# A host layout by channel for the input of a two-layer encoder kernel, with token norms from TensorE sums

## Chip, cores and metric

The kernel runs on one core of a Trainium2 chip. The metric is the device time of one execution in microseconds (us); for the kernel before it is 1353.13 us, the median of 3 runs (1353.13 to 1354.86).

## What is computed

A trunk of two layers on 1040 tokens (16 learned meta tokens ahead of 1024 inputs, the padding in front of them left out by the kernel) of 1024 channels, in float32. The first layer is a gated DeltaNet: a token norm, one projection to queries, keys, values, gate and two small per-head vectors (b and a), a causal convolution of 4 taps per channel, SiLU, and a chunkwise recurrence. The second is a multi-head latent attention. The change concerns the first lines:

```python
def rms_norm(x, g):
    xf = x.astype(jnp.float32)
    y = xf * lax.rsqrt(jnp.mean(xf * xf, -1, keepdims=True) + EPS)
    return (y * g.astype(jnp.float32)).astype(x.dtype)

def deltanet_layer(x, valid, g_norm, w_in, conv_w, a_log, dt_bias, o_gain, w_out):
    ...
    h = jnp.where(valid[None, :, None], rms_norm(x, g_norm), 0)
    z = h @ w_in
    qkv = jax.nn.silu(causal_dwconv(z[..., :2 * DN_KW + DN_VW], conv_w))
    gate = z[..., 2 * DN_KW + DN_VW:2 * DN_KW + 2 * DN_VW]
    b_raw = z[..., 2 * DN_KW + 2 * DN_VW:2 * DN_KW + 2 * DN_VW + DN_HEADS].astype(jnp.float32)
    a_raw = z[..., 2 * DN_KW + 2 * DN_VW + DN_HEADS:].astype(jnp.float32)
    ...
```

## The kernel before

The normalised input is held by channel: `hT_hi` and `hT_lo` hold, for each of 8 channel tiles of 128 (`kt`), all 1040 tokens. Each number is split into a high part that TensorE takes in its rounded float32 type and a low remainder; a product of two split operands is three TensorE products (`mm3`, lines 91 to 93). The tokens go in three chunks, `TOKC`, of 272, 384 and 384.

*The input stage (lines 215 to 259).* Ten small loads on SP's queue bring x for the first tiles and the norm gains and convolution taps; a TensorE transpose turns these parameters into columns (`pcol`, line 237). For each of 9 token tiles (16 tokens, then 8 of 128) ScalarE squares and sums (`xs`, line 250, through `act`, line 82), a short Newton step on VectorE and ScalarE gives the inverse root (`rsqrt`, lines 173 to 178), and Pool scales the rows (line 252). Then, for each chunk and channel tile, TensorE transposes (line 258), ScalarE writes the high part (line 110) and VectorE the low part (line 111), both with the gain.

*The a/b projection and the gates (lines 261 to 337).* 48 products (lines 274, 275) on all chunks, then a short row of steps on VectorE and ScalarE, and the decay sums on TensorE (lines 325 to 328).

*The projection columns.* `load_w` (line 197) loads a column of 128 outputs in two halves into `raw` (two buffers); Pool writes its high part `whi` (line 98) and VectorE its low part `wlo` (line 99), two buffers each. `conv_acts` multiplies one column with the three chunks (24 x 3 products), ScalarE copies to `z` (line 370, two buffers), Pool and VectorE convolve (lines 372, 375), ScalarE applies SiLU. The order of the columns is keys of heads 0 and 1, values 0 and 1 (one buffer for their result), queries 0 and 1, and so on by pairs of heads. Between them stands the key preparation of a pair (lines 385 to 465, with products of keys with keys at line 440 and masks from Pool at line 429), and the inverse of small blocks on VectorE (line 519 on).

*What sets the order.* A scheduler orders each engine's instructions when the kernel is built, by the program's order and by what it expects to be ready; on the chip each engine takes its instructions in that order. SP's queue issues all loads and stores in its own order, and a load whose buffer is not free holds those behind it. ScalarE has two tables in use, one for Ln and Exp and one for SiLU; `act` orders the steps so that a table is changed only where the program's order changes it: no SiLU of the keys before the gates' last Exp, and no Ln or Exp of the key preparation before the keys' last SiLU.

Of the kernel before, what the change touches and what calls it, by code (L numbers as in the profile page):

```python
# [23 lines left out]
P = 128  # L24
D = 1024
# [14 lines left out]
PART = count()  # L40
TOKC = [(0, 272), (272, 656), (656, 1040)]
# [75 lines left out]
def body(ctx: ExitStack, tc: tile.TileContext, I, out):  # L117
# [37 lines left out]
    off = {}  # L155
    pcol = ctile("pcol", [P, P])

    def col(key, k=0):
        c = off[key] + k
        return pcol[:, c:c + 1]  # L160
# [21 lines left out]
    with ExitStack() as la:  # L182
# [12 lines left out]
        w_in = I["a_w_in"][0].rearrange("(kt p) c -> p kt c", p=P)  # L195

        def load_w(c0):
# [16 lines left out]

        with ExitStack() as l0:
            xp = l0.enter_context(tpool(name="x0", bufs=2))

            def load_x(t):
                a, b = tok(t)
                xt = xp.tile([P, D], F32, tag="xt", name=nm("xt"), bufs=3)  # L220
                SY.dma_start(xt[:b - a], I["meta_tokens"] if t < 0 else I["x"][0, t * P:(t + 1) * P, :])
                return xt

            xts = {t: load_x(t) for t in (-1, 0, 1)}
            n = 0
            prow = xp.tile([P, P], F32, tag="prow", name="prow", bufs=1)
            for key, src, k in (("a", I["a_norm"][0], 8), ("kv", I["kv_norm"], 8), ("b", I["b_norm"][0], 8),
                                ("og", I["a_o_gain"][0], 1), ("gl", I["kv_latent_norm"], 2),
                                ("gq", I["b_q_latent_norm"][0], 3), ("kg", I["k_gain"][0:NOPE], 1),
                                ("qg", I["b_q_gain"][0, 0:NOPE], 1)):  # L230
                SY.dma_start(prow[n:n + k, :], src.rearrange("(k p) -> k p", p=P))
                off[key] = n
                n += k
            SY.dma_start(prow[n:n + 96, :], I["a_conv"][0].rearrange("j (m p) -> (j m) p", p=P))
            off["cw"] = n
            ptp = bank("tr", [P, 512])
            TE.transpose(ptp[:, 0:P], prow, ident)
            V.tensor_copy(pcol, ptp[:, 0:P])
            V.tensor_tensor(out=gg, in0=col("kg"), in1=col("qg"), op=ALU.mult)
            V.tensor_scalar(out=gg, in0=gg, scalar1=QK ** -0.5, scalar2=None, op0=ALU.mult)  # L240
            for c, (a, b) in enumerate(TOKC):
                tiles = [t for t in range(-1, NT) if a <= tok(t)[0] < b]
                xss = []
                for t in tiles:
                    r0, r1 = tok(t)
                    k = r1 - r0
                    xt = xts.pop(t) if t in xts else load_x(t)
                    xs = xp.tile([P, D], F32, tag="xs", name=nm("xs"), bufs=5)
                    ss = xp.tile([P, 1], F32, tag="ss", name=nm("ss"), bufs=4)
                    act(xs[:k], xt[:k], AF.Square, accum_out=ss[:k])  # L250
                    rsqrt(ss[:k], ss[:k], 1.0 / D, EPS)
                    G.tensor_scalar(out=xs[:k], in0=xt[:k], scalar1=ss[:k], scalar2=1.0,
                                    op0=ALU.mult, op1=ALU.mult)
                    xss.append((xs, r0, k))
# [92 lines left out]
        for h0 in range(0, H, 2):  # L347
            order += [2 * D + h0 * P, 2 * D + (h0 + 1) * P, h0 * P, (h0 + 1) * P]
            if h0 + 2 < H:
                order += [D + (h0 + 2) * P, D + (h0 + 3) * P]  # L350
# [1119 lines left out]
```

## Time and profile before

| | |
|---|---|
| median of 3 runs | 1353.13 us (1353.13 to 1354.86) |
| the profiled execution | 1351.8 us |
| its span, first to last instruction | 1350.1 us |
| TensorE busy | 1306.3 us, 97% |
| VectorE busy | 900.1 us, 67% |
| ScalarE busy | 534.8 us, 40% |
| Pool busy | 412.8 us, 31% |
| mean granted TensorE clock | 0.989 |

PE is TensorE's product, PEld its weight load, DVE VectorE, ACT ScalarE, POOL GpSimd (Pool here), SP the queue that issues loads and stores. A busy TensorE is not TensorE at its peak: products are pipelined, so the distance between two starts, not the duration of one, tells what each costs. All numbers below come from the one profiled execution.

### The profile page before, as it was taken

The numbers are of one execution on the slowest core, as the hardware profiler recorded it, in microseconds if no ns is written. First come the engines' busy times: TensorE is split into PE (matmuls) and PEld (weight loads), VectorE is DVE, ScalarE is ACT, GpSimd is POOL, SyncE is SP. The second block draws the span as 40 slices with busy tenths as digits, with TensorE's granted clock in tenths as the row PEclk, the third lists the DMA queues.
The fourth block names the chain that finished last, engine by engine and source line by source line (L and its number), as shares of the span: only waits on it lengthen the run. The fifth ranks groups of instructions, "written<-read, shape, count | busy, mean of one in ns | idle before, by whom it ended". The sixth has DMA issues, their size and how long they took to land.

```text
span 1350.1 us, 24895 instructions
## 1 busy us (share of the span) xinstructions
PE 1306.3 (97%) x9064; PEld 1181.7 (88%) x9064; DVE 900.1 (67%) x2601; ACT 534.8 (40%) x1694; POOL 412.8 (31%) x680
## 2 busy tenths in 40 slices
PE   6999999999999999999999999998999999998998
PEld 4879989989998999997888798887999999998876
DVE  6669879968978884633553765224888878788221
ACT  6442343244325322211222243116777677776100
POOL 3344224323421320060101402212535435347000
PEclk9999999999999999999999999999999999999999
DMA  6111202111211113255441302311111101014443
GB/s 185 41 25 48 56 20 62 40 42 37 59 49 32 50 32 96 72 159 178 145 147 68 95 1 84 121 47 57 44 38 35 56 21 36 21 36 149 133 124 125
DMA packets 116924, 96.81 MB, mean 72 GB/s; under 512 B 28462, under 2 KB 106094, under 8 KB 116802
## 3 DMA queue, kind: packets, MB, share of 16 engines
q1 hardware_dynamic: 116802, 95.23, 23.7%
q8 instruction: 71, 1.16, 0.4%
q14 instruction: 51, 0.42, 0.1%
HBM read 68.19 MB, written 27.01 MB: 71 GB/s over the span
## 4 chain that ended last, share of the span: by engine, by line
PE 75%; DVE 8%; DMA 5%; POOL 5%; ACT 4%; issue 3%; SPq 0%; DVEq 0%; ACTq 0%; POOLq 0%
PE mm L91 7%; PE mm L93 7%; PE mm L92 7%; PE sc L93 6%; PE sc L92 6%; PE sc L91 6%; PE bd L91 3%; PE bd L93 3%; PE bd L92 3%; PE pt L1312 2%; PE tr L483 1%; DMA raw<-in_a_w_out 1%; ACT junk L82 1%; DMA out<-raw 1%; PE ch L625 1%
## 5 line engine op out<-in xcount | busy, mean ns | idle before, releaser
L91 PE MATMUL mm<-hT_hi,whi 128*128 128x384 f32 (+1 forms) x768 | 256.8, 334 | 3.5 <-DVE whi L98 3.5
L93 PE MATMUL mm<-hT_hi,wlo 128*128 128x384 f32 (+1 forms) x768 | 255.3, 332 | 0.7 <-DVE wlo L99 0.7
L92 PE MATMUL mm<-hT_lo,whi 128*128 128x384 f32 (+1 forms) x768 | 255.7, 333 | 0.0
L91 PEld LDWEIGHTS mm<-hT_hi,whi 128*128 128x128 f32 x768 | 147.4, 192 | 5.5 <-issue 4.7
L93 PEld LDWEIGHTS mm<-hT_hi,wlo 128*128 128x128 f32 x768 | 147.5, 192 | 2.5 <-DVE wlo L99 1.3
L92 PEld LDWEIGHTS mm<-hT_lo,whi 128*128 128x128 f32 x768 | 147.2, 192 | 1.4 <-issue 0.4
L108 DVE TENSOR_TENSOR pTl<-pt,pTh 128x256 fp32r<-128x256 f32 (+2 forms) x112 | 55.0, 494 | 11.0 <-ACT pTh L107 9.5
L98 POOL TENSOR_SCALAR whi<-raw 128x512 fp32r<-128x512 f32 x48 | 37.7, 799 | 70.4 <-PE mm L92 63.8
L82 ACT ACTIVATE P<-P,mx 128x144 f32<-128x144 f32 (+3 forms) x64 | 50.6, 791 | 21.8 <-DVE mx L1270 19.0
L91 PE MATMUL sc<-wo_hi,oTh 128*128 128x512 f32 (+1 forms) x144 | 57.5, 400 | 0.6 <-issue 0.6
L93 PE MATMUL sc<-wo_hi,oTl 128*128 128x512 f32 (+1 forms) x144 | 57.2, 397 | 0.0
L92 PE MATMUL sc<-wo_lo,oTh 128*128 128x512 f32 (+1 forms) x144 | 56.9, 395 | 0.0
L375 DVE SCALAR_TENSOR_TENSOR kn<-z,pcol,kn 128x384 f32<-128x384 f32 (+1 forms) x72 | 41.4, 576 | 19.4 <-POOL kn L372 18.8
L1283 POOL TENSOR_SCALAR P<-P,sl 128x144 f32<-128x144 f32 (+3 forms) x64 | 53.0, 829 | 3.7
L370 ACT COPY z<-mm 128x384 f32<-128x384 f32 (+1 forms) x72 | 31.8, 442 | 54.4 <-PE mm L93 54.3
L107 ACT CAST pTh<-pt 128x256 fp32r<-128x256 f32 (+2 forms) x112 | 47.3, 427 | 14.1 <-PE pt L1312 8.0
L99 DVE TENSOR_TENSOR wlo<-raw,whi 128x512 fp32r<-128x512 f32 x64 | 47.1, 746 | 8.5 <-POOL whi L98 8.4
L93 PE MATMUL sc<-h_hi,wlo 128*128 128x512 f32 x128 | 50.8, 397 | 0.0
L92 PE MATMUL sc<-h_lo,whi 128*128 128x512 f32 x128 | 50.6, 396 | 0.0
L91 PE MATMUL sc<-h_hi,whi 128*128 128x512 f32 x128 | 50.5, 395 | 0.0
L91 PE MATMUL bd<-wf_hi,oTh 128*128 128x512 f32 x128 | 50.2, 392 | 0.3 <-ACT oTh L1422 0.2
L102 DVE SCALAR_TENSOR_TENSOR wlo<-raw,pcol,whi 128x128 fp32r<-128x128 f32 x64 | 23.4, 429 | 40.0 <-POOL whi L101 40.0
(380 smaller groups left out, 3951.1 us busy)
## 6 DMA issues: line engine op xcount, KB each, us to landing
raw<-in_a_w_in SPq DMA_DIRECT2D x64, 256.0 KB
xt<-in_x SPq DMA_DIRECT2D x16, 512.0 KB
o_scr<-o SPq DMA_DIRECT2D x64, 64.0 KB
raw<-in_a_w_out SPq DMA_DIRECT2D x8, 512.0 KB
on<-o_scr SPq DMA_DIRECT2D x8, 512.0 KB
x_scr<-xt SPq DMA_DIRECT2D x8, 512.0 KB
raw<-in_b_w_in SPq DMA_DIRECT2D x8, 512.0 KB
gb_scr<-z SPq DMA_DIRECT2D x8, 512.0 KB
```

What stands on the lines that cost most here:

```text
L82: i = A.activation(out_ap, in_ap, func, **kw)
L91: TE.matmul(ps, ahi, bhi, start=first, stop=False)
L92: TE.matmul(ps, ahi, blo, start=False, stop=False)
L93: TE.matmul(ps, alo, bhi, start=False, stop=last)
L98: eng.tensor_scalar(out=hi, in0=raw, scalar1=1.0, scalar2=1.0, op0=ALU.mult, op1=ALU.mult)
L99: V.tensor_tensor(out=lo, in0=raw, in1=hi, op=ALU.subtract)
L107: A.copy(hi, ps)
L108: V.tensor_tensor(out=lo, in0=ps, in1=hi, op=ALU.subtract)
L370: A.copy(z[:, 3 + a:3 + b], gemm_T(hi, lo, c))
L375: V.scalar_tensor_tensor(out=yc, in0=z[:, a + j:b + j], scalar=col("cw", 24 * j + m), in1=yc, op0=ALU.mult, op1=ALU.add)
L1283: G.tensor_scalar(out=Pm[:, 0:n], in0=Pm[:, 0:n], scalar1=s, scalar2=1.0, op0=ALU.mult, op1=ALU.mult)
L1312: TE.transpose(pt[:, kb, x * P:(x + 1) * P], Ps[x][0][:, y0 + kb * P:y0 + (kb + 1) * P], ident)
```

## The change

The host now hands over three arrays laid out by channel: x with the meta tokens (`x_t`, per partition the 8 channel tiles of one chunk side by side), the projection weights (`a_w_in`, per column of 128 outputs a block with 128 partitions, and `a_w_ab` for the small projection) and all gains and taps as columns. The kernel loads x in halves of a chunk straight into the channel layout. The square sums over channels are formed by TensorE, as products of a matrix of ones with the squares, which leaves each token's sum on all partitions; from chunk 1 on Pool first adds the upper four squared channel tiles to the lower four, so that 4 products do instead of 8. The Newton step then works on whole 128-partition tiles, one per chunk. VectorE multiplies x by gain and norm in place, ScalarE copies the high part and VectorE subtracts for the low part. The transposes of x and of the parameters are gone. The loads of the first two weight columns are put between the loads of x; the order list and `weights` move up for that without a change.

```diff
@@ load_w
-        w_in = I["a_w_in"][0].rearrange("(kt p) c -> p kt c", p=P)
+        w_in = I["a_w_in"]
...
-                SY.dma_start(raw, w_in[:, s4, c0:c0 + P])
+                SY.dma_start(raw, w_in[c0 // P, :, s4])
@@ input stage
+        wab = hp.tile([P, KT, 2 * H], F32, name="wab")
         with ExitStack() as l0:
-            xp = l0.enter_context(tpool(name="x0", bufs=2))
-
-            def load_x(t):
-                a, b = tok(t)
-                xt = xp.tile([P, D], F32, tag="xt", name=nm("xt"), bufs=3)
-                SY.dma_start(xt[:b - a], I["meta_tokens"] if t < 0 else I["x"][0, t * P:(t + 1) * P, :])
+            xp = l0.enter_context(tpool(name="x0", bufs=1))
+
+            def load_x(c):
+
+                a, b = TOKC[c]
+                w = b - a
+                xt = xp.tile([P, KT, w], F32, tag=f"xt{c}", name=nm("xt"))
+                for q in range(0, KT, 4):
+                    SY.dma_start(xt[:, q:q + 4], I["x_t"][:, KT * a + q * w:KT * a + (q + 4) * w].rearrange(
+                        "p (k w) -> p k w", w=w))
                 return xt
 
-            xts = {t: load_x(t) for t in (-1, 0, 1)}
...
+            xts = {0: load_x(0)}
+            SY.dma_start(pcol, I["columns"])
+            ready[order[0]] = load_w(order[0])
+            SY.dma_start(wab, I["a_w_ab"])
+            xts[1] = load_x(1)
+            ready[order[1]] = load_w(order[1])
+            xts[2] = load_x(2)
             V.tensor_tensor(out=gg, in0=col("kg"), in1=col("qg"), op=ALU.mult)
             V.tensor_scalar(out=gg, in0=gg, scalar1=QK ** -0.5, scalar2=None, op0=ALU.mult)
             for c, (a, b) in enumerate(TOKC):
...
+                xt, w = xts[c], b - a
+
+                sq = xp.tile([P, KT, 384], F32, tag="sq", name=nm("sq"))[:, :, 0:w]
+                ps = bank("tr", [P, 512])[:, 0:w]
+                n = KT
+                for q in range(0, KT, 4):
+                    act(sq[:, q:q + 4], xt[:, q:q + 4], AF.Square)
+                if c > 0:
+                    n = KT // 2
+                    G.tensor_tensor(out=sq[:, 0:n], in0=sq[:, 0:n], in1=sq[:, n:KT], op=ALU.add)
+                for kt in range(n):
+                    TE.matmul(ps, ones, sq[:, kt], start=kt == 0, stop=kt == n - 1)
+                sh, y, t = (xp.tile([P, 384], F32, tag=x, name=nm(x), bufs=2)[:, 0:w] for x in ("xsh", "xy", "xn"))
+                V.tensor_scalar(out=sh, in0=ps, scalar1=-0.5 / D, scalar2=-0.5 * EPS, op0=ALU.mult, op1=ALU.add)
+                act(y, sh, AF.Ln, scale=-2.0)
+                act(y, y, AF.Exp, scale=-0.5)
+                V.tensor_tensor(out=t, in0=y, in1=y, op=ALU.mult)
+                V.tensor_tensor(out=t, in0=t, in1=sh, op=ALU.mult)
+                V.scalar_tensor_tensor(out=y, in0=t, scalar=1.5, in1=y, op0=ALU.add, op1=ALU.mult)
                 for kt in range(KT):
-                    ps = bank("tr", [P, 512])
-                    for xs, r0, k in xss:
-                        TE.transpose(ps[:, r0 - a:r0 - a + k], xs[:k, kt * P:(kt + 1) * P], ident[:k, :k])
-                    split_ps(ps[:, 0:b - a], hT_hi[:, kt, a:b], hT_lo[:, kt, a:b], col("a", kt))
+                    f, hi, lo = xt[:, kt], hT_hi[:, kt, a:b], hT_lo[:, kt, a:b]
+                    V.scalar_tensor_tensor(out=f, in0=f, scalar=col("a", kt), in1=y, op0=ALU.mult, op1=ALU.mult)
+                    A.copy(hi, f)
+                    V.tensor_tensor(out=lo, in0=f, in1=hi, op=ALU.subtract)
@@ arrays_of (host)
+    x = np.concatenate([inputs["meta_tokens"], inputs["x"][0]]).T.reshape(KT, P, L)
+    arrays["x_t"] = np.concatenate(
+        [np.ascontiguousarray(x[:, :, a:b].transpose(1, 0, 2)).reshape(P, -1) for a, b in TOKC], axis=1)
...
+    w = np.asarray(inputs["a_w_in"])[0].reshape(KT, P, -1)
+    arrays["a_w_in"] = np.ascontiguousarray(w[:, :, :4 * D].reshape(KT, P, 4 * KT, P).transpose(2, 1, 0, 3))
+    arrays["a_w_ab"] = np.ascontiguousarray(w[:, :, 4 * D:].transpose(1, 0, 2))
```

## Rows read from the trace of the kernel before

**Rows 1.** the page: busy time of each engine, and the chain by engine

```profile
PE 1306.3 (97%) x9064; PEld 1181.7 (88%) x9064; DVE 900.1 (67%) x2601; ACT 534.8 (40%) x1694; POOL 412.8 (31%) x680
...
PE 75%; DVE 8%; DMA 5%; POOL 5%; ACT 4%; issue 3%; SPq 0%; DVEq 0%; ACTq 0%; POOLq 0%
```

**Rows 2.** busy time by stage (PE, PEld, DVE, ACT, POOL), granted clock, DMA

```profile
0.00:11.00 11.00, 1.72 (x6) 0.93 (x6) 4.49 (x20) 5.97 (x14) 4.61 (x13) 1.00 0.53 174
11.00:62.00 51.00, 47.31 (x277) 39.21 (x277) 35.08 (x87) 26.35 (x68) 16.84 (x25) 0.97 0.35 101
62.00:103.00 41.00, 38.51 (x240) 32.58 (x239) 28.41 (x86) 17.86 (x67) 19.69 (x36) 1.00 0.16 39
103.00:153.00 50.00, 50.00 (x330) 49.01 (x330) 48.03 (x117) 12.21 (x28) 17.29 (x24) 0.97 0.16 40
```

**Rows 3.** chain of work, 0 to 30 us; columns: start us, us, what

```profile
1.24 3.67 DMA xt<-in_x
...
10.35 3.81 PE tr L258 x13
...
16.76 0.23 PE fin L274
...
19.39 0.12 PE fin L274
```

**Rows 4.** chain of work, 30 to 64 us

```profile
41.41 0.33 PE tr L258 x3
...
62.31 1.20 POOL whi L98 x2
```

**Rows 5.** timeline of TensorE; start us, us, engine, line, operation, tiles, shapes

```profile
33.19 0.33 PE L92 MATMUL mm<-hT_lo,whi 128*128 128x384 f32 x1
...
33.36 0.34 PE L93 MATMUL mm<-hT_hi,wlo 128*128 128x384 f32 x1
...
76.17 0.83 PE L440 MATMUL tr<-kn 128*128 128x128 f32 x6
...
77.20 0.61 PE L440 MATMUL tr<-kn 128*128 128x128 f32 x4
```

**Rows 6.** timeline of SP's queue

```profile
13.54 1.64 SPq L203 DMA_DIRECT2D raw<-in_a_w_in  x2
```

**Rows 7.** TensorE by line and shape, 60 to 82 us; count, busy, mean

```profile
L440 PE MATMUL tr<-kn 128*128 128x128 f32 x16 | 2.4, 275 | 0.0
```

**Rows 8.** groups of ScalarE by line and shape, 0 to 53.3 us

```profile
L82 ACT ACTIVATE xs<-xt 128x1024 f32<-128x1024 f32 x8 | 8.4, 1054 | 0.2 <-DMA xt<-in_x 0.2
```

**Rows 9.** groups of VectorE by line and shape, 0 to 53.3 us

```profile
L111 DVE SCALAR_TENSOR_TENSOR hT_lo<-tr,pcol,hT_hi 128x384 fp32r<-128x384 f32 x16 | 9.2, 612 | 4.5 <-ACT hT_hi L110 4.4
...
L111 DVE SCALAR_TENSOR_TENSOR hT_lo<-tr,pcol,hT_hi 128x272 fp32r<-128x272 f32 x8 | 3.8, 498 | 1.7 <-ACT hT_hi L110 1.6
...
L178 DVE SCALAR_TENSOR_TENSOR ss<-nt,ny 128x1 f32<-128x1 f32 x8 | 2.8, 353 | 0.2
```

**Rows 10.** timeline of VectorE, one weight remainder

```profile
104.09 0.68 DVE L99 TENSOR_TENSOR wlo<-raw,whi 128x512 fp32r<-128x512 f32 x1
```

**Rows 11.** groups of Pool by line and shape, whole span

```profile
L98 POOL TENSOR_SCALAR whi<-raw 128x512 fp32r<-128x512 f32 x48 | 37.7, 799 | 70.4 <-PE mm L92 63.8 <-DMA raw<-in_a_w_in 6.6
...
L1407 POOL TENSOR_TENSOR wf_lo<-raw,wf_hi 128x1024 fp32r<-128x1024 f32 x4 | 9.5, 2377 | 2.0 <-ACT wf_hi L1406 2.0
```

**Rows 12.** timelines: last input step, K1's last convolution step, table load

```profile
42.66 0.61 DVE L111 SCALAR_TENSOR_TENSOR hT_lo<-tr,pcol,hT_hi 128x384 fp32r<-128x384 f32 x1
...
66.37 0.62 DVE L375 SCALAR_TENSOR_TENSOR kn<-z,pcol,kn 128x384 f32<-128x384 f32 x1
...
67.55 1.28 ACT L79 ACT_TABLE_LOAD   x1
```

**Rows 13.** timeline of Pool, the same step twice

```profile
44.54 0.58 POOL L372 TENSOR_SCALAR kn<-z,pcol 128x384 f32<-128x384 f32 x1 [7.05 <-ACT z L370]
...
63.50 1.53 POOL L372 TENSOR_SCALAR kn<-z,pcol 128x384 f32<-128x384 f32 x1
```

More of the change, by code (lines that the diff above doesn't have):

```diff
@@ L40 @@
 PART = count()
+COL = {"a": 0, "kv": 8, "b": 16, "og": 24, "gl": 25, "gq": 27, "kg": 30, "qg": 31, "cw": 32}
+COLUMNS = 128
 TOKC = [(0, 272), (272, 656), (656, 1040)]
@@ L152, in body @@
     one = ones[:, 0:1]
-    off = {}
-    pcol = ctile("pcol", [P, P])
+    pcol = ctile("pcol", [P, COLUMNS])
     def col(key, k=0):
-        c = off[key] + k
+        c = COL[key] + k
         return pcol[:, c:c + 1]
@@ L213, in gemm_T @@
             return ps
-        with ExitStack() as l0:
-            xp = l0.enter_context(tpool(name="x0", bufs=2))
-            def load_x(t):
-                a, b = tok(t)
-                xt = xp.tile([P, D], F32, tag="xt", name=nm("xt"), bufs=3)
-                SY.dma_start(xt[:b - a], I["meta_tokens"] if t < 0 else I["x"][0, t * P:(t + 1) * P, :])
-                return xt
-            xts = {t: load_x(t) for t in (-1, 0, 1)}
[L225 to L238, printed above, removed]
@@ new lines, in body, with weights @@
+        order = [D, D + P]
+        for h0 in range(0, H, 2):
+            order += [2 * D + h0 * P, 2 * D + (h0 + 1) * P, h0 * P, (h0 + 1) * P]
+            if h0 + 2 < H:
+                order += [D + (h0 + 2) * P, D + (h0 + 3) * P]
+        order += [3 * D + h * P for h in range(H)]
+        ready = {}
+        def weights(c0):
+            n = order.index(c0)
+            for c in order[n:n + 2]:
+                if c not in ready:
+                    ready[c] = load_w(c)
+            return ready.pop(c0)
@@ L241, in body @@
             for c, (a, b) in enumerate(TOKC):
[L242 to L254, printed above, removed]
+                xt, w = xts[c], b - a
@@ L261, in body @@
+                    A.copy(hi, f)
+                    V.tensor_tensor(out=lo, in0=f, in1=hi, op=ALU.subtract)
         with ExitStack() as l0:
             ap_ = l0.enter_context(tpool(name="ab", bufs=1, side="right"))
-            wab = ap_.tile([P, KT, 2 * H], F32, tag="wab", name="wab", bufs=1)
-            SY.dma_start(wab, w_in[:, :, 4096:4096 + 2 * H])
             wab2 = ap_.tile([P, KT, 2, 2 * H], F32R, tag="wab2", name="wab2", bufs=1)
@@ L342, in body @@
         bp = ld.enter_context(tpool(name="bA", bufs=1))
-        order = [D, D + P]
[L347 to L350, printed above, removed]
-        order += [3 * D + h * P for h in range(H)]
-        ready = {}
-        def weights(c0):
-            n = order.index(c0)
-            for c in order[n:n + 2]:
-                if c not in ready:
-                    ready[c] = load_w(c)
-            return ready.pop(c0)
         def conv_acts(c0, tag, bufs):
@@ L1453, in arrays_of @@
     arrays["rope_cos"], arrays["rope_sin"] = rope_tables()
+    x = np.concatenate([inputs["meta_tokens"], inputs["x"][0]]).T.reshape(KT, P, L)
[4 more added lines that the diff above has]
+    arrays["a_w_ab"] = np.ascontiguousarray(w[:, :, 4 * D:].transpose(1, 0, 2))
+    rows = {"a": inputs["a_norm"][0], "kv": inputs["kv_norm"], "b": inputs["b_norm"][0], "og": inputs["a_o_gain"][0],
+            "gl": inputs["kv_latent_norm"], "gq": inputs["b_q_latent_norm"][0], "kg": inputs["k_gain"][:NOPE],
+            "qg": inputs["b_q_gain"][0, :NOPE], "cw": inputs["a_conv"][0]}
+    arrays["columns"] = np.ascontiguousarray(
+        np.concatenate([np.asarray(rows[key]).reshape(-1, P) for key in COL]).T)
     return arrays
```

5 lines of the change are left out of this document (2 added, 3 removed).

## Prediction

> **What bounds the kernel now.** I read four views, from the whole to the place. First the page's busy times and its chain of work that ended last: TensorE is busy for 97% of the span, and three quarters of the chain is its own work [rows 1]. A microsecond saved elsewhere is worth nothing unless TensorE waits for it. Second, a table of stages: between 11 and 62 us VectorE is busy 35.1 of 51 us and TensorE 47.3; between 103 and 153 us TensorE is busy all the time and VectorE 48.0 of 50 [rows 2]. So a second engine is near its limit soon behind the change. Third, the chain of the first 30 us, where the change lies. The reader is to see that "busy" flatters TensorE there: up to about 19 us its instructions come at half rate. [...] The column of the granted clock does not show it (0.97 from 11 to 62 us [rows 2]); the spacing does. Fourth, the timeline, for spacings and for where the stage ends.
>
> I take as the stage's end the moment when the first two projection columns, the keys of heads 0 and 1 (K0 and K1 here, each 24 products on each of three token chunks), are through. In the chain that is 62.31 us, when Pool may write weights into the buffer that K1 frees [rows 4]. What TensorE needs up to there at the full clock: 64 full transposes at 0.11 us = 7.0; 8 small ones, about 0.8; the a/b projection, 16 products at 0.12 and 32 at 0.17 us = 7.4; K0 and K1, 48 at 0.12 and 96 at 0.17 = 22.1; some 2 for the decay sums, an estimate. That is 39.3 us (272 columns cost 0.12 [rows 3], 384 cost 0.17, from 33.19 to 33.36 us [rows 5]). TensorE starts just before the transposes of 10.35 us [rows 3], about 9 us, so 53 us pass and some 14 are lost: to the low clock, to waits for normalised rows, and to the weights, whose load is issued at 13.54 us, behind all parameters [rows 6].
>
> **The change part by part.**
>
> *TensorE's own work is not reduced.* The 72 transposes go (7.8 us). The sums of squares come: 8 products of 272 columns in chunk 0, 4 of 384 in each other chunk. They are plain fp32, and such a product is two instructions: the 8 products of 128 columns of line 440 appear as 16 [rows 7], and six instructions take 0.83 us where four take 0.61, 0.11 us each [rows 5]. By columns that is 0.23 us for 272 and 0.33 for 384, so 16 x 0.23 + 16 x 0.33 = 9.0 us: 1.2 us more than before, and 3.7 us more still if chunk 0's run at the low clock. A gain can come only from the 14 lost us.
>
> *Loads.* x arrives in two pieces a chunk, 4.3 or 6.1 KB per partition; nine parameter loads become one; the first weights stand right behind chunk 0. The first x tile now lands 3.67 us after its issue [rows 3]; I take 4.3 us for the first half chunk and 6 for the second. The second weight column waits on SP's queue until Pool and VectorE have split the first (about 10 us), and x chunk 2 is queued behind it there: 1.6 MB later, at 16 to 18 us. It is needed at about 23 us, which hides it; without that cover each us late would count in full.
>
> *Chunk 0.* ScalarE squares 1088 columns twice, about 1.1 us each by the 1.05 us for 1024 [rows 8], ready at 6.9 us. The 16 passes run 3.7 us at the full clock and 7.4 at the lower; TensorE starts idle, so I take the sums at 12 us (10.5 to 13). Then a scaling, Ln, Exp and three VectorE steps on 272 columns, about 3.2 us with their waits: the norm y at 15.2. Now for each of 8 channel tiles one scaling of two tensors, 0.50 us like the present 272-column step [rows 9], ScalarE's copy beside it (its 384-column copy is hidden behind VectorE today too), and one subtraction of two SBUF tensors. For that the ends are the 512-column row by columns, 0.68 us [rows 10] giving 0.36 and 0.51, and the present steps, 0.50 and 0.61 [rows 9]; I take 0.44 and 0.55, between them, since a row has a fixed part. So 0.94 us x 8 = 7.5: chunk 0 ends at 22.7.
>
> *Chunks 1 and 2.* The squares share one buffer, free when chunk 0's products have read it (12 us); 2 x 1.6 us on ScalarE; then Pool adds 1536 columns of two tensors. Pool's nearest row is 2.38 us for 1024 [rows 11], so 3.6 us (its ends: rival C). Products 2.6, norm 4: y of chunk 1 at about 27. Then 8 x (0.61 + 0.55) = 9.3 us, to 36.5. Chunk 2's sums are ready by then; its norm costs 3 us, its steps 9.3: **input ready at 49 us (46 to 55)**. In the kernel before it is ready at 43.3, the end of the last step of line 111 [rows 12]. So the input itself comes 5 to 6 us later.
>
> *Why the stage can still end earlier.* K0 and K1 follow each channel tile behind VectorE (six products of 0.12 or 0.17 us each), with their weights there from the start. From 16.5 us: 7.4 + 22.1 + 5.2 (sums of chunks 1 and 2) = 34.7 us, and 2 to 4 more for the low clock and gaps: 53 to 56 us against 62.3, a lead of 6 to 9 us for TensorE.
>
> *What is late next: VectorE.* Removed are 24 steps of line 111, 9.2 + 3.8 us, and nine token norms of four steps, of which line 178 is 2.8 us [rows 9]; with its three sister lines and the parameter copy I estimate 8. Added are 24 scalings (13.8), 24 subtractions (12.3) and three norms (6.3). That is 32.4 - 21 = 11 to 12 us more. The cover is VectorE's idle time, 15.9 us between 11 and 62 and 12.6 between 62 and 103 [rows 2]. Next on the path is K1's last convolution step at 66.37 us and ScalarE's table load at 67.55, behind which the key preparation stands [rows 12]. VectorE was busy 39.6 us up to 62 us [rows 2]; less 21, plus 32.4, plus 3.6 for K1's last steps and one weight remainder, less 2.5 that lies early: 52 us from 12.5 on, with 1 to 4 idle, so 66 to 69 us. This path is level, between 1 us early and 2 late, while TensorE stands 6 to 9 us ahead.
>
> *How much of the lead is kept.* TensorE may run on into the first values column: its z buffer is free once K0 is convolved, about 58 us. It may not run on forever: the fourth column from there needs a z that waits for the values' convolution, which waits, through the table order and a single values buffer, for the key preparation of both heads. Between 62 and 103 us VectorE has 12.6 us idle, much of it waiting for what TensorE delivers; so about half of the lead should last, 3 to 5 us. Past 103 us TensorE bounds again and carries what is left to the end. I take 4. The profiled execution lasted 1351.8 us (span 1350.1), 1.3 under the median of 1353.13; the gain is taken from the median: **1349 us**.
>
> *Weight tiles by channel* (2 KB runs for 512 B) act on 64 loads. Weights wait for a buffer more than for the transfer: of Pool's 70.4 idle us before them, 63.8 end with a product and 6.6 with a load [rows 11]. Worth 0, at most 1 us.
>
> [...] The row shows transposes from 10.35 us on without the full clock, and the rise only by 19.39, behind 2.6 us of products [rows 3]. [...]
>
> **The rivals.**
>
> *B, lead given back (1352.5, 1350.5 to 1355.5).* The key preparation starts level, and TensorE, out of z buffers, waits for it. For: VectorE is 48.0 of 50 us busy from 103 on. Against: its 12.6 idle us before. Price: the 4 us are gone, some small change stays.
>
> *C, slower (1357, 1355.8 to 1361).* Pool's add stretches beside VectorE's steps on two SBUF tensors. Pool's 384-column step takes 0.58 us at 44.54 and 1.53 at 63.50, beside such steps [rows 13], 2.6 times. An add of 3.6 us would be 9.4, 5.8 more; of chunk 1's delay VectorE fills 2 us with other work, chunk 2's is hidden behind chunk 1's steps. Input at 53 to 55, the key path 4 us late, TensorE's lead spent. It decides from about 6 us per add on. Against: Pool's four two-tensor steps, 9.5 us together [rows 11], lie beside VectorE work too and may already be as slow as it gets. [...]
>
> *D, it does not do what it says (1353).* TensorE, paced by VectorE from the start, stays at the low clock and ends K1 at 62 again. Counted with B.
>
> **How the numbers follow.** Forecast A (1349, 1343 to 1350.4) 0.48; B with D 0.30; C 0.22. About 0.2%, 2.7 us, is what a measurement of this kernel can tell from no change, so faster 0.48, same 0.30, slower 0.22. The range is from 1343 (the whole lead kept and the full clock early; less than a tenth below) to 1358 (a tenth above).
>
> **What would show it.** Right: input ready at 46 to 52 us, K1's buffer free at 53 to 56, VectorE over 90% busy from 15 to 60, the adds 3.6 us, the table load at 64 to 69. Wrong: adds over 6 us; TensorE idle for more than 3 us between 60 and 110; K1 at 60 or later; sums of chunk 0 after 14 us. A lead that is larger at 150 us than at 60 would make my path through VectorE wrong.

## Result, and the profile after

The changed kernel takes 1356.64 us (median of 20 runs) where the kernel before took 1352.09 beside it (20 runs): ratio 1.0037, 95% interval 1.0024 to 1.0051. It is slower by about 5 us; 1349 was forecast. The profiled execution of the changed kernel lasted 1359.81 us, 3.2 above its own median, so its span (1358.1 us) overstates the difference by that much.

Page of the changed kernel: busy times, and shares of the chain by engine.

```profile
PE 1304.8 (96%) x9023; PEld 1179.7 (87%) x9023; DVE 912.4 (67%) x2600; ACT 535.1 (39%) x1670; POOL 410.4 (30%) x673
...
PE 68%; DVE 12%; ACT 5%; issue 5%; DMA 5%; POOL 4%; SPq 0%; ACTq 0%; DVEq 0%; POOLq 0%
```

Against [rows 1], TensorE's busy time falls by 1.5 us and VectorE's rises by 12.3. That is near the 11 to 12 us of the prediction by luck: 6.2 us of it are not work but the two held steps shown below. VectorE's share of the chain goes from 8 to 12%. The table of stages shows where (columns as in [rows 2]).

```profile
0.00:11.00 11.00, 5.08 (x11) 3.87 (x12) 3.43 (x10) 3.50 (x3) 3.29 (x13) 1.00 0.83 302
11.00:62.00 51.00, 37.16 (x187) 28.34 (x186) 42.66 (x79) 21.88 (x41) 13.23 (x10) 0.87 0.18 63
62.00:103.00 41.00, 37.86 (x233) 32.27 (x232) 31.02 (x92) 19.16 (x73) 20.44 (x37) 1.00 0.15 43
103.00:153.00 50.00, 48.47 (x322) 47.04 (x320) 46.71 (x107) 15.09 (x34) 19.75 (x29) 1.00 0.13 41
```

Between 11 and 62 us TensorE is busy 37.2 us where it was 47.3 [rows 2], and its granted clock falls from 0.97 to 0.87. VectorE is busy 42.7 of 51 us instead of 35.1, and part of that is not work. The timeline of VectorE in the first 37 us (start us, us, engine, line, operation, tiles, shapes, and in brackets the idle time before it and what ended it):

```profile
16.00 0.44 DVE L276 SCALAR_TENSOR_TENSOR xy<-xn,xy 128x272 f32<-128x272 f32 x1
16.48 3.71 DVE L279 SCALAR_TENSOR_TENSOR xt<-xt,pcol,xy 128x272 f32<-128x272 f32 x1
...
30.75 3.54 DVE L274 TENSOR_TENSOR xn<-xy 128x384 f32<-128x384 f32 x1 [0.89 <-ACT xy L84]
...
35.09 0.56 DVE L276 SCALAR_TENSOR_TENSOR xy<-xn,xy 128x384 f32<-128x384 f32 x1
```

and Pool's timeline in the same stretch:

```profile
16.48 3.42 POOL L267 TENSOR_TENSOR sq<-sq 128x1536 f32<-128x1536 f32 x1 [2.89 <-ACT sq L84]
...
30.45 3.44 POOL L267 TENSOR_TENSOR sq<-sq 128x1536 f32<-128x1536 f32 x1 [9.78 <-ACT sq L84]
```

Read the two together. A VectorE step of 0.44 to 0.56 us takes 3.71 and 3.54 us, and each ends as Pool's add does (16.48 + 3.42 = 19.90 against 20.19; 30.45 + 3.44 = 33.89 against 34.29). VectorE stands for 6.2 us in two pieces. TensorE waits from 8 to 62 us (us in total, times, longest) for VectorE's tiles, which ScalarE copies (first row), and once for the sum of Pool's second add (second row):

```profile
PE fin L294 <- ACT hT_hi L280: 10.1, 2, 8.0
PE tr L269 <- POOL sq L267: 2.8, 1, 2.8
```

The 8.0 us are one gap, from 12.7 to 20.7 us, with the first held step within it. Two stretches of ten microseconds show the clock that TensorE is granted around that gap; the columns are those of the table of stages.

```profile
10.00:20.00 10.00, 2.66 (x8) 1.69 (x7) 5.48 (x6) 3.61 (x4) 4.14 (x3) 0.75 0.82 283
20.00:30.00 10.00, 9.05 (x41) 6.28 (x42) 8.50 (x20) 6.11 (x11) 0.67 (x1) 0.74 0.21 77
```

Products are slower there too. The eight passes of chunk 1's sums lie in the stretch with 0.74 and take 4.46 us, where chunk 2's eight, at a granted clock of 1.00 from 30 to 40 us, take 2.85:

```profile
21.84 4.46 PE L269 MATMUL tr<-sq,ones 128*128 128x384 f32 x8
...
33.94 2.85 PE L269 MATMUL tr<-sq,ones 128*128 128x384 f32 x8 [2.79 <-POOL sq L267]
```

How the delay goes on is seen from four marks: the last input step (VectorE), K0's and K1's weight buffer rewritten (Pool), and the table load ahead of the key preparation (ScalarE).

```profile
53.94 1.09 DVE L281 TENSOR_TENSOR hT_lo<-xt,hT_hi 128x384 fp32r<-128x384 f32 x2
```

```profile
57.72 1.65 POOL L100 TENSOR_SCALAR whi<-raw 128x512 fp32r<-128x512 f32 x2 [10.75 <-PE mm L94]
69.60 1.60 POOL L100 TENSOR_SCALAR whi<-raw 128x512 fp32r<-128x512 f32 x2 [0.59 <-PE mm L94]
```

```profile
75.34 1.28 ACT L81 ACT_TABLE_LOAD   x1
```

Against [rows 4] and [rows 12]: the input is ready at 55.0 us instead of 43.3, K1's buffer is free at 69.60 instead of 62.31 (+7.3), the table load comes at 75.34 instead of 67.55 (+7.8). The first step of the block inversions, one large VectorE instruction, then starts 7.9 us late; in the changed kernel and in the kernel before:

```profile
115.79 1.21 DVE L521 TENSOR_TENSOR M<-M,bb 66x1024 f32<-66x1024 f32 x1
...
107.94 1.21 DVE L519 TENSOR_TENSOR M<-M,bb 66x1024 f32<-66x1024 f32 x1
```

The next inversion starts at 227.1 against 219.3 (+7.8). So the delay arises before 70 us, and from there it is carried along.

The marks of all kernels, read from the same views, for the next section (ratio to the kernel before, with its interval; for the last three kernels K1 is free at the end of its last product, since Pool can come to the buffer later):

| kernel | input ready, us | K1 free, us | table load, us | first inversion, us | ratio |
|---|---|---|---|---|---|
| before | 43.3 | 62.31 | 67.55 | 107.94 | 1 |
| changed | 55.0 | 69.60 | 75.34 | 115.79 | 1.0037 [1.0024, 1.0051] |
| no add | 45.5 | 60.63 | 66.28 | 106.19 | 0.9961 [0.9941, 0.9980] |
| idle add | 51.6 | 66.73 | 72.39 | 112.30 | 0.9999 [0.9982, 1.0016] |
| idle one-tensor step | 47.5 | 62.56 | 68.22 | 108.14 | one run, 1346.38 us |
| add in four | 53.6 | 66.71 | 72.44 | 112.88 | 1.0034 [1.0018, 1.0051] |
| add on VectorE | 55.2 | 69.43 | 75.15 | 115.58 | 1.0048 [1.0031, 1.0065] |
| weights alone | 42.2 | 61.30 | 66.54 | 107.19 | 1.0005 [0.9990, 1.0021] |
| fp32r sums | 47.4 | 60.48 | 66.20 | 106.82 | 0.9956 [0.9940, 0.9973] |
| three buffers | 45.8 | 60.91 | 66.73 | 111.51 | 1.0082 [1.0068, 1.0096] |
| fp32r, three buffers | 46.9 | 59.99 | 65.75 | 113.97 | 1.0228 [1.0214, 1.0242] |
| changed, by chunks | 55.5 | 63.6 | 72.88 | 114.64 | 1.0082 [1.0056, 1.0108] |
| no add, by chunks | 46.0 | 57.0 | 64.39 | 107.31 | 0.9944 [0.9923, 0.9965] |
| fp32r, by chunks | 44.7 | 51.2 | 62.59 | 104.30 | 0.9955 [0.9927, 0.9983] |

One caution for all that follows. The scheduler lays the order down anew for every kernel, so a small edit can reorder the engines' instructions far behind it. Two pairs of traces have nearly the same order on all engines: no add and idle add (TensorE's orders differ at eight instructions), and no add and idle one-tensor step. The weights alone keep the order of the kernel before unchanged. In every other pair compared below the order differs over long stretches, so a difference in time is the edit's and the order's together.

### The profile page after: what moved, and what is told of

Same layout as the page of the kernel before. It is cut to its first block, busy times and chain, and to the rows that moved or that the text cites. A ratio compares the mean times of both kernels' runs of the same rounds, so it can differ in the third digit from the quotient of the medians.

```text
span 1358.1 us, 24748 instructions
## 1 busy us (share of the span) xinstructions
PE 1304.8 (96%) x9023; PEld 1179.7 (87%) x9023; DVE 912.4 (67%) x2600; ACT 535.1 (39%) x1670; POOL 410.4 (30%) x673
## 4 chain that ended last, share of the span: by engine, by line
PE 68%; DVE 12%; ACT 5%; issue 5%; DMA 5%; POOL 4%; SPq 0%; ACTq 0%; DVEq 0%; POOLq 0%
PE sc L95 6%; PE sc L94 6%; PE sc L93 6%; PE mm L93 6%; PE mm L94 6%; PE mm L95 6%; PE bd L93 4%; PE bd L95 4%; PE bd L94 4%; PE pt L1314 2%; ACT junk L84 1%; DMA raw<-in_b_w_out 1%; DVE qT L377 1%; PE tr L485 1%; PE po L95 1%
## 5 line engine op out<-in xcount | busy, mean ns | idle before, releaser
L1283 POOL TENSOR_SCALAR Pe<-P,sl 128x128 f32<-128x128 f32 x64 | 28.7, 449 | 79.2 <-DVE sl L1280 56.9
```

What stands on the lines that cost most here:

```text
L1283: G.tensor_scalar(out=Pe, in0=Pm[:, None, 0:NM].broadcast_to([P, E8, NM]), scalar1=s, scalar2=1.0, op0=ALU.mult, op1=ALU.mult)
```

## Experiments

**Is it the add?** The theory after the two traces: Pool's two-tensor add holds VectorE's two-tensor steps for its whole length (H). The rival: the loss comes from waiting for the add's result, the sum (W). A third theory: the input is late because of TensorE's low clock, 0.87 granted from 11 to 62 us (L). First the add is taken away.

```diff
-                if c > 0:
-                    n = KT // 2
-                    G.tensor_tensor(out=sq[:, 0:n], in0=sq[:, 0:n], in1=sq[:, n:KT], op=ALU.add)
```

> The changed kernel without Pool's add: all three chunks form their sums with 8 products. Its trace shows one VectorE step of 3.71 us (line 279, others 0.45) and one of 3.54 (line 274, others 0.56), each as long as Pool's add beside it (3.42 and 3.44 us). Theory H (held): Pool's add of two SBUF tensors holds VectorE's two-tensor step for its whole length. Then no VectorE step between 12 and 50 us is over 1.2 us; the input is ready at 47 to 50 us instead of 55.0 (6.2 us of stalls and 3.4 us of one add less, 2.6 us of products more), K1's buffer is free at 61 to 64.5 instead of 69.6, and the ratio to the kernel before is 0.998 to 1.001. [...]

Ratio 0.9961, 1345.61 us against 1351.34: 0.4% faster than the kernel before, a larger gain than the 0.998 to 1.001 expected. No VectorE step is held; the stage's row reads:

```profile
11.00:62.00 51.00, 47.43 (x258) 37.20 (x257) 44.05 (x97) 25.51 (x53) 10.33 (x18) 1.00 0.22 73
```

TensorE is busy 10 us more of this stretch than in the changed kernel and its granted clock is 1.00. The input is ready at 45.5 us, earlier than the 47 to 50 expected, and K1 is free at 60.63 us, just before the 61 to 64.5. This run alone can't tell H from W: without an add there is no wait for it either. Nor does it rule out the low clock (L), since the granted clock rose as well.

**The add without its result.** The sum goes over all eight tiles, as above, and Pool makes the same add into a tile that nothing reads.

```diff
+                    spare = xp.tile([P, KT // 2, 384], F32, tag="spare", name=nm("spare"))
+                    G.tensor_tensor(out=spare, in0=sq[:, 0:4], in1=sq[:, 4:8], op=ALU.add)
```

> As the run without the add, but Pool still makes the same add of 1536 columns, from chunk 1 on, into a spare tile that nobody reads; the sums take all 8 products. Theory H: two VectorE steps of about 3.5 us are back though nobody waits for the add; input 3 to 7 us later than without the add (51 to 55), ratio 0.002 to 0.004 above that run. Theory W (the add costs only because its result is waited for): no step over 1.2 us, times as without the add within 0.001.

Ratio 0.9999. Nobody waits for the sum, and VectorE is held again. VectorE:

```profile
16.08 3.72 DVE L279 SCALAR_TENSOR_TENSOR xt<-xt,pcol,xy 128x272 f32<-128x272 f32 x1
...
27.25 3.43 DVE L281 TENSOR_TENSOR hT_lo<-xt,hT_hi 128x272 fp32r<-128x272 f32 x1
```

Pool:

```profile
16.07 3.42 POOL L267 TENSOR_TENSOR spare<-sq 128x1536 f32<-128x1536 f32 x1 [2.60 <-ACT sq L84]
...
26.93 3.45 POOL L267 TENSOR_TENSOR spare<-sq 128x1536 f32<-128x1536 f32 x1 [6.66 <-ACT sq L84]
```

The granted clock stays at 1.00, so the low clock (L) isn't needed for the delay:

```profile
11.00:62.00 51.00, 43.17 (x222) 31.84 (x221) 46.59 (x88) 22.48 (x44) 13.07 (x12) 1.00 0.21 69
```

Two more things are seen here. The step held is whichever comes next: in chunk 2 it is another line than in the changed kernel. And the delay is passed on whole at first: input +6.1 us, K1 +6.1, first inversion +6.1 against the kernel without the add, whose instructions stand in nearly the same order; at the end 1350.41 against 1345.61, 4.8 us. H is shown, and W isn't needed for these 4.8 us.

That the changed kernel takes 5 us more again (1.0037 against 0.9999) is not explained by H. Its K1 comes 2.9 us later than here. Three things differ there: TensorE waits 2.8 us for the second add's sum (W); chunk 1's sums, which here run at 13.89 us ahead of chunk 0's first a/b product (20.30 us), stand behind it in the changed kernel, so that TensorE idles for 8 us in one piece; and they then run at the lower clock (0.74 from 20 to 30 us). No run takes these three apart, and some 2 of the 5 us arise behind K1, where the order differs too.

What a VectorE step does that reads one operand from PSUM is seen late in the changed kernel, beside a Pool step on two SBUF tensors. Pool, then VectorE:

```profile
1253.79 2.38 POOL L1409 TENSOR_TENSOR wf_lo<-raw,wf_hi 128x1024 fp32r<-128x1024 f32 x1
...
1254.22 1.29 DVE L110 TENSOR_TENSOR pTl<-pt,pTh 128x512 fp32r<-128x512 f32 x2 [0.38 <-ACT pTh L109]
```

VectorE's two steps run inside Pool's one and take their usual 0.69 us each: `pt` lies in PSUM, and neither step is held.

**Two tensors or one?** In place of the idle add, an idle copy of one tensor.

```diff
-                    G.tensor_tensor(out=spare, in0=sq[:, 0:4], in1=sq[:, 4:8], op=ALU.add)
+                    G.tensor_scalar(out=spare, in0=sq[:, 0:4], scalar1=1.0, scalar2=1.0,
+                                    op0=ALU.mult, op1=ALU.mult)
```

> The changed kernel without the add in the sum (all eight channel tiles go through TensorE), and instead of the idle add a Pool step that reads one tensor only: 1536 columns of the squares copied into a spare tile that nothing reads. If any Pool work of this length holds VectorE, one VectorE step in each of chunks 1 and 2 takes as long as the Pool step (1.7 us or more, by Pool's one-tensor split of 512 columns at 0.6 to 0.7 us), and the input is ready 2 to 4 us later than in the run without the add (45.5 us). If it is the form that reads two tensors that holds, every VectorE step keeps its 0.42 to 0.56 us (the fp32r split its 0.6 to 0.8), the Pool step takes 1.2 to 2.3 us, and the input is ready at 45 to 47 us.

Pool:

```profile
13.24 1.47 POOL L267 TENSOR_SCALAR spare<-sq 128x1536 f32<-128x1536 f32 x1 [3.16 <-ACT sq L84]
14.67 1.57 POOL L100 TENSOR_SCALAR whi<-raw 128x512 fp32r<-128x512 f32 x2
21.37 3.17 POOL L267 TENSOR_SCALAR spare<-sq 128x1536 f32<-128x1536 f32 x1 [5.13 <-ACT sq L84]
```

VectorE:

```profile
13.97 1.03 DVE L275 TENSOR_TENSOR xn<-xy 128x272 f32<-128x272 f32 x1 [1.91 <-ACT xy L84]
15.03 0.73 DVE L276 TENSOR_TENSOR xn<-xn,xsh 128x272 f32<-128x272 f32 x1
...
23.13 1.70 DVE L280 SCALAR_TENSOR_TENSOR xt<-xt,pcol,xy 128x272 f32<-128x272 f32 x1
```

So "two tensors only" falls: here a Pool step on one tensor held VectorE too, for what was left of it. The 0.44 us step at 13.97 ends 0.3 us after the copy does (14.71), and the 0.50 us step at 23.13 ends after the second copy (24.54). That copy itself takes 3.17 us instead of 1.47: it was issued while VectorE's two-tensor steps ran, and waited 1.7 us for them, some four of VectorE's steps, which came back to back. Here each stood for the other, whichever came first, and a row of VectorE's steps without a break kept Pool out for more than one of them. The changed kernel has this more strongly at 130.64 us, where a Pool step on one tensor that can take 0.58 us [rows 13] takes 3.74 beside such a row, while VectorE's steps keep their lengths:

```profile
130.64 3.74 POOL L374 TENSOR_SCALAR qT<-z,pcol 128x384 f32<-128x384 f32 x1 [0.68 <-ACT z L372]
```

The input is 2.0 us later than without the copy. The harm of the add is its length, 3.42 us against 1.47 for the same 1536 columns.

**The same add in four pieces.**

```diff
-                    G.tensor_tensor(out=sq[:, 0:n], in0=sq[:, 0:n], in1=sq[:, n:KT], op=ALU.add)
+                    for j in range(n):
+                        G.tensor_tensor(out=sq[:, j], in0=sq[:, j], in1=sq[:, n + j], op=ALU.add)
```

> The changed kernel with Pool's add cut into four instructions of 384 columns in place of one of 1536 (3.42 us, so 0.86 us each and some start time). If a VectorE step that reads two SBUF tensors stands for as long as the one Pool instruction runs, then none takes over 1.5 us now; how much VectorE loses in all tells how the two share. If they take turns instruction by instruction, VectorE still loses nearly the length of the adds (5 to 7 us in all, spread over some eight steps), the input is ready at 53 to 56 us (55.0 with one instruction), and the ratio stays at 1.002 to 1.005. If long instructions alone are the harm, VectorE loses 2 us or less, the input is ready at 49 to 52 us, and the ratio is 0.998 to 1.001.

VectorE, beside four adds that Pool needs 4.80 us for in chunk 2:

```profile
29.89 1.05 DVE L275 TENSOR_TENSOR xn<-xy 128x384 f32<-128x384 f32 x1 [0.87 <-ACT xy L84]
30.97 1.23 DVE L276 TENSOR_TENSOR xn<-xn,xsh 128x384 f32<-128x384 f32 x1
32.24 1.23 DVE L277 SCALAR_TENSOR_TENSOR xy<-xn,xy 128x384 f32<-128x384 f32 x1
```

They take turns. No step takes over 1.5 us, but each of the last two pays 0.67 us on top of its 0.56, and the input is ready at 53.6 us. The ratio is 1.0034, as with one instruction. Cutting the instruction did not give VectorE its time back: the input comes 1.4 us sooner than with one instruction (55.0), and 8.1 us later than without the add (45.5).

**The add on VectorE instead.**

```diff
-                    G.tensor_tensor(out=sq[:, 0:n], in0=sq[:, 0:n], in1=sq[:, n:KT], op=ALU.add)
+                    V.tensor_tensor(out=sq[:, 0:n], in0=sq[:, 0:n], in1=sq[:, n:KT], op=ALU.add)
```

> The changed kernel with the add on VectorE instead of Pool. [...] Theory W or L: input at 53 to 56, ratio 1.003 or above.

By H I looked for a smaller loss than with the add on Pool. A miss: ratio 1.0048, input at 55.2 us. The add is half as long (1.76 us), but it now stands in VectorE's own queue:

```profile
23.18 1.76 DVE L267 TENSOR_TENSOR sq<-sq 128x1536 f32<-128x1536 f32 x1
...
28.38 0.56 DVE L271 TENSOR_SCALAR xsh<-tr 128x384 f32<-128x384 f32 x1 [3.09 <-PE tr L269]
...
31.68 1.76 DVE L267 TENSOR_TENSOR sq<-sq 128x1536 f32<-128x1536 f32 x1 [2.41 <-ACT sq L84]
```

The 3.09 and 2.41 us of idle time are what I had left out: VectorE waits for chunk 1's sums, then stands at chunk 2's add, which waits for ScalarE's squares, while chunk 1's norm is queued behind it. Together with the adds they cost VectorE as much as the held steps did: the input comes at the same time, 55.2 against 55.0 us.

**The weight layout alone**, on the kernel before (the small projection's weights and the host's side change with it and are not shown).

```diff
-                SY.dma_start(raw, w_in[:, s4, c0:c0 + P])
+                SY.dma_start(raw, w_in[c0 // P, :, s4])
```

> The kernel before with one part of the change alone: the projection weights and the a/b weights laid out on the host in the blocks that are loaded, everything else (token-major input, transposes, weight loads after the input) as before. The first 62 us of the kernel before show no wait of TensorE for a weight; the loads are shorter but nobody waits for them there. Theory: the layout of the weights is worth nothing, ratio 0.998 to 1.001, K1's buffer free at 61.5 to 62.5 us as before. The rival, that part of the gain of the kernel without the add (ratio 0.996) comes from shorter weight loads anywhere in the first 570 us, needs a ratio of 0.997 or less.

Ratio 1.0005, K1 free at 61.30 us, 1.0 us earlier than in the trace of the kernel before and just before the 61.5 to 62.5 expected. At the end the layout moves no more than the measurement tells, which is in line with the prediction's 0 to 1 us.

**The sums in one pass.** No add, and squares and ones in fp32r, so that a product is one instruction instead of two.

```diff
-                sq = xp.tile([P, KT, 384], F32, tag="sq", name=nm("sq"))[:, :, 0:w]
+                sq = xp.tile([P, KT, 384], F32R, tag="sq", name=nm("sq"))[:, :, 0:w]
...
-                    TE.matmul(ps, ones, sq[:, kt], start=kt == 0, stop=kt == n - 1)
+                    TE.matmul(ps, ones_r, sq[:, kt], start=kt == 0, stop=kt == n - 1)
```

> The changed kernel without the add, with the squares and the ones in TensorE's rounded float32 type: one instruction for each product and a quarter of the time. The sums are of squares rounded to that type. Theory H with a second point B (K1 cannot run beside the input, since the two PSUM buffers of the projection go to K0's chunks in order): chunk 0's sums ready at 9 to 10 us instead of 12.7, no VectorE step over 1.2 us, input ready at 42 to 46, K0 done 2 to 3 us later and K1 11 to 12 us after that, its buffer free at 56 to 60; ratio 0.995 to 0.998, which is faster than the kernel before. Theory L: with the low clock as the bound, input at 47 or later, ratio 0.999 or above.

Ratio 0.9956, not to be told from the kernel without the add (0.9961). At the half rate of the first 20 us an fp32r product of 272 columns takes 0.23 us (from start to start, in the a/b projection at 17.75 to 18.66 us), and a plain one in the changed kernel two instructions of 0.45: a quarter of the time, as expected. Chunk 0's sums take 2.65 us instead of 6.22 there, and its norm starts 3.7 us sooner, but the input is ready at 47.4 us and K1 is free at 60.48, outside the 42 to 46 and the 56 to 60 expected. VectorE stands between the chunks, in chunk 1's norm above all:

```profile
23.49 0.53 DVE L273 TENSOR_TENSOR xn<-xy 128x384 f32<-128x384 f32 x1
25.40 0.56 DVE L270 TENSOR_SCALAR xsh<-tr 128x384 f32<-128x384 f32 x1 [1.38 <-PE tr L268]
25.87 0.55 DVE L274 TENSOR_TENSOR xn<-xn,xsh 128x384 f32<-128x384 f32 x1
...
37.76 0.55 DVE L295 COPY abT<-fin 32x384 f32<-32x384 f32 x1 [1.70 <-PE fin L294]
```

Chunk 2's first step (25.40) stands between chunk 1's first and second and waits for TensorE. Later, chunk 1's a/b copy (37.76) stands between the steps of chunk 2's norm and waits too, as chunk 0's did just before these rows (1.76 us). The order of the queue, fixed before the run, eats what the shorter sums gave: 4.8 us in these three waits. The granted clock is lower too (0.97 over the first 200 us, against 0.98 without the add); its share is not told apart.

**Why does K1 not run beside the input?** In the changed kernel K1's chunks 1 and 2 come behind K0's last one. My theory was that the two PSUM buffers of the projections force this; so a third one, taken from the transposes.

```diff
-            return pp.tile(shape, F32, tag=tag, name=nm(tag), bufs={'mm': 2, 'tr': 3, 'fin': 1, 'ch': 2}[tag])
+            return pp.tile(shape, F32, tag=tag, name=nm(tag), bufs={'mm': 3, 'tr': 2, 'fin': 1, 'ch': 2}[tag])
```

On the kernel without the add:

> The kernel without the add, with one PSUM buffer taken from the transposes ('tr' 3 to 2) and given to the projections ('mm' 2 to 3). Theory: it is the two 'mm' buffers that keep K1 behind K0, so that with three K1's chunk 0 runs before the last chunk of the input is ready, and K1's weight buffer is free at 57 to 60 us (60.6 with two), ratio to before 0.993 to 0.996. If the order of the products is set by something else (when the input is ready, or TensorE being full in that stretch) K1's buffer stays at 60 to 61.5 us, and the ratio is 0.995 to 0.999; later than 62 would say that the key preparation misses the third transpose buffer.

and the same edit on the kernel with fp32r sums, with two buffers for the squares as well ("one pass of TensorE instead of four" holds by time, 0.23 us against 0.90 for 272 columns as above; by instructions it is one for two):

> The kernel with the sums of squares in fp32r and without the add, with three 'mm' and two 'tr' buffers as in the run beside it, and two buffers for the squares. The sums take one pass of TensorE instead of four, so TensorE has room for K1 beside the input, and squares of the next chunk do not wait for the sums of the last. If both limits are what they seem, the input is ready at 43 to 46 us, K1's buffer is free at 54 to 58 us, and the ratio to before is 0.990 to 0.994. If VectorE's queue alone sets the pace, the input stays at 46 to 48 us, K1 at 59 to 61, and the ratio at 0.995 to 0.997.

K1 stays where it was (60.91 against 60.63, 59.99 against 60.48): the theory falls. The ratios, 1.0082 and 1.0228, come later: behind 62 us TensorE waits, in the first of the two, 5.2 us at transposes for VectorE's reading of the last ones, a wait that the kernel without the add does not show.

```profile
PE tr L501 <- DVE vb L497: 5.2, 4, 2.3
```

It seems that the third transpose buffer is needed there. The edit's whole price (16 us against the kernel without the add) is more than this wait; the rest I did not follow up.

**The order as it is written.** K0 and K1 chunk by chunk: both on chunk 0, then on chunk 1, then on chunk 2.

(An excerpt; `conv_steps` is `conv_acts` with a yield behind each chunk.)

```diff
-        keys_of(0)
-        keys_of(1)
+        s0, hs[0]["kn"] = conv_steps(D, "kn", 4)
+        s1, hs[1]["kn"] = conv_steps(D + P, "kn", 4)
+        for _ in zip(s0, s1):
+            pass
```

In the changed kernel:

> The changed kernel whole, the add on Pool with it, but the products of the first two key heads written chunk by chunk (K0 and K1 of chunk 0, then of chunk 1, then of chunk 2) where K0's three chunks stood ahead of K1's. Theory: TensorE runs its products in the order in which they were laid down before the run, and K1's chunks 1 and 2 stand there behind K0's last one, so they wait for the input to be ready (55.0 us) though their own tiles were there. With this order K1's chunk 1 (24 products of 384 columns at 0.175 us, 4.2 us) runs before 55 us, and K1's weight buffer is free at 63.5 to 66.5 us instead of 69.60; input ready unchanged at 54 to 56 us; ratio 0.999 to 1.002 where the changed kernel had 1.0037. If the order of writing does not reach TensorE's queue, or the input's end alone sets K1, the buffer stays at 69 to 71 us and the ratio at 1.003 to 1.005.

without the add:

> The same order chunk by chunk in the kernel without the add. There TensorE is busy 47.4 of the 51 us from 11 to 62, so at most 3.6 us can be drawn forward: K1's buffer free at 57 to 60 us (60.63 without), K0's buffer later than its 49 us, ratio 0.993 to 0.996 (0.9961 without). If K1's time comes only from how much TensorE has to do, the ratio does not differ from 0.996.

and with fp32r sums:

> The same order in the kernel with the sums of squares in fp32r and no add, where TensorE has some 8 us of room before the input is ready (47.4 us). K1's buffer free at 55 to 58 us (60.48 without), ratio 0.991 to 0.995 (0.9956 without). Against it: TensorE may stand for VectorE, which works without a break up to the end of the input, and then nothing is gained.

Now the order reaches TensorE. In the changed kernel K1's second chunk is copied out before the input is ready (55.5 us), and K1 is through at 63.6 us instead of 69.6; ScalarE's copies of K1's chunk 1, K0's chunk 2 and K1's chunk 2:

```profile
53.95 0.48 ACT L379 COPY z<-mm 128x384 f32<-128x384 f32 x1
...
59.45 0.48 ACT L379 COPY z<-mm 128x384 f32<-128x384 f32 x1 [4.61 <-PE mm L95]
...
63.67 0.48 ACT L379 COPY z<-mm 128x384 f32<-128x384 f32 x1 [0.26 <-PE mm L95]
```

In the other two K1 is through at 57.0 and 51.2 us. But the three gains of 6.0, 3.6 and 9.3 us shrink to 2.5, 1.9 and 3.6 at the table load, and at the first inversion to 1.2 early, 1.1 late and 2.5 early. The ratios are 1.0082 (worse than the changed kernel's, against my 0.999 to 1.002), 0.9944 and 0.9955, the last two level with the kernels they come from. In these three pairs a lead of TensorE at K1 is mostly gone by then, while the delay between no add and idle add was passed on whole. The first kernel is 1.2 us ahead at the first inversion, so its loss arises later; its runs also have a lower clock (median over the run 0.982, the changed kernel's 0.987). I have not traced it further. The order of the instructions behind K1 differs within each pair, so the runs do not show that the key preparation alone takes the leads back.

The best kernels of this study are those without the add and with two projection buffers: 0.9944 to 0.9961, intervals that overlap.

## Why the prediction was wrong

**The step that failed** is that of chunks 1 and 2: "Pool adds 1536 columns of two tensors ... 3.6 us", with VectorE going on beside it. The add's length was right, 3.42 and 3.44 us. What the prediction left out is that a VectorE step on two SBUF tensors stood beside each add, 3.71 and 3.54 us for 0.44 to 0.56. The sum had no term for that, and it was 6.2 us. Alone, with a sum that nobody waits for, such an add cost 4.8 us at the end; the used one costs about 10 (1.0037 against 0.9961), and how the other 5 divide over the wait for the sum, the clock and the order stays open. Rival C had the right place and the wrong direction: I let Pool's add stretch beside VectorE's steps, from Pool's 384-column step, 0.58 and 1.53 us [rows 13], while the add, once begun, kept its 3.42 to 3.45 us and VectorE's step was stretched. C's counter-argument, Pool's unstretched two-tensor steps of 2.4 us [rows 11], did not bear on it, since the VectorE subtractions beside them read one operand from PSUM, and those kept their 0.69 us. Stretch and standstill were one behaviour in the one-tensor copy: 1.47 us where it came first and 3.17 where VectorE did. [rows 13] was a sign of taking turns, and should have been priced on both engines. C's time (1357) was near the measured one, by other steps: the input at 55.0 us and the key path 7.8 us late instead of 4.

So the rows show the hold in both directions (3.71 us for 0.45, 3.17 for 1.47), and one thing beside it: Pool waited for more than one VectorE step where they came without a break.

**Point by point.**

- *TensorE's work not reduced*: right. Without the add the 16 passes of a 384-column chunk take 5.43 us, and TensorE is busy 47.4 us from 11 to 62 us, against 47.3 before.
- *Sums of chunk 0 at 12 us (10.5 to 13)*: 12.70 us; the passes took 6.74 us, near the 7.4 for the low clock. A rise within chunk 0 did come, but too late to bring the sums forward: the passes start 0.45 us apart up to 11.5 us and 0.23 apart from 11.8 on, for the last three of the 16. By the low clock the prediction means this half rate: in the kernel before, an a/b product took 0.23 us at 16.76 us and 0.12 at 19.39 [rows 3], and a transpose 0.11 at 41.41 [rows 4]. No view gives a frequency.
- *y of chunk 1 at about 27 us*: 35.65. Its own terms (12 + 3.2 + 3.6 + 2.6 + 4) add up to 25.4, not 27. Ahead of it the trace has TensorE's gap of 8 us, with the first hold in it, and the second hold.
- *Input ready at 49 us (46 to 55)*: 55.0, its upper end. Less the two holds it is 48.8, and the run without the add gave 45.5.
- *K1's buffer free at 53 to 56 us*: wrong by more than the holds explain, 69.60, and still 60.63 without the add. "K0 and K1 follow each channel tile" is what failed: TensorE's order is fixed before the run, and K1's chunks 1 and 2 stand behind K0's last one. Written chunk by chunk, and with sums of one pass, K1 was through at 51.2 us.
- *Key path level, table load at 66 to 69 us*: 75.34; without the add 66.28, in the range. VectorE's sum was too high, not right: without the add its busy time is 907.5 us, 7.4 over the kernel before, where 11 to 12 were expected.
- *Half of TensorE's lead is kept, 4 us*: not confirmed. Leads of 3.6 to 9.3 us at K1 were worth -1.1 to 2.5 us at the first inversion, and the kernels with the lead ended no better than those they came from. On this step the runs side with rival B (the lead is given back), though no view here shows TensorE out of z buffers.
- *The forecast time*: the kernel without the add has a ratio of 0.9961, and 1349 over 1353.13 is 0.997. That is no proof of my steps. At the first inversion that kernel is only 1.7 us ahead, and the other 4 us come behind 340 us (it is 1.3 behind at the second inversion, 0.7 ahead at the third, 3.8 at the fourth). Its order of work differs from that of the kernel before on all engines. I had no term for it, and which of the reordered pieces gains it stays open.
- *Weight tiles by channel, 0 to 1 us*: in line, 1.0005 [0.9990, 1.0021], which can't tell 0 from 1 us.

**What stays open.** The delay of 7.8 us at the first inversion is 4.6 us between the medians. Part of what is measured is the clock: the mean granted clock of a run is 0.987 in the median of the changed kernel's runs and 0.989 in that of the kernel before. Among runs at 0.988, the spans are 1354.0 us (median of 5) and 1351.2 (16, from the later comparisons), 2.8 apart. So, as an estimate, some 3 us belong to the program and some 1 to 2 to the clock. Whether the clock is lower because TensorE stands more in the first 60 us, no run tells.

## What to carry to other kernels

Before work goes to Pool "beside" VectorE, list what VectorE runs at that time: beside steps on two SBUF tensors one engine stood here while the other worked, with the add in one instruction (3.71 us for a step of 0.45) and in four (1.23 for 0.56). A long Pool step stopped VectorE; a row of VectorE steps without a break stopped Pool (3.74 us for 0.58). A step is free on an idle engine only if it leaves the engine that paces the stage alone. A gain ahead of a later stage can end there, as it did here between K1 and the first inversion, while a delay went through: price the two apart. And to show what one instruction costs, compare kernels whose instruction order is otherwise the same, as the idle add and the kernel without it.

## What the runs showed of the hardware

- Pool's instructions on SBUF tensors and VectorE's steps on two SBUF tensors stood for each other in these traces: 3.72 us for a step of 0.45 beside an add of 3.42 us, 1.23 for 0.56 beside adds of a quarter of that, 3.17 for a Pool copy of 1.47. Beside a row of VectorE steps without a break Pool stood for more than one of them (3.74 us for 0.58). VectorE steps that read one operand from PSUM ran unheld inside a Pool step on two SBUF tensors (0.69 us each, Pool's 2.38).
- For 1536 fp32 columns Pool took 3.42 us to add two tensors and 1.47 to copy one; VectorE added the two in 1.76.
- The granted clock fell to 0.75 between 10 and 20 us and 0.74 between 20 and 30, around the stretch in which TensorE stood for 8 us; eight passes took 4.46 us there and 2.85 later. The kernels without the add and with the idle add had 1.00 from 11 to 62 us.
